# An eight-core decoder trunk: the first FFN on unnormalised input, ordered start DMAs, and the even mixer block by block

## The chip, the cores and the metric

The kernel runs on all 8 cores of one Trainium2 chip, in two dies of four cores. Each core computes one prompt of 2048 tokens and 16 sampled sequences of 8 tokens; the cores don't talk to one another. The metric is the device time of the slowest core in microseconds (us).

A program on all cores has a second, slower state: in some executions the cores of one die, or of both, get a lower TensorE clock (one run of start_only took 3130 us, with the cores of one die at 0.83). Only fast runs are compared here. Quoted ratios are the mean time of one kernel's fast runs over that of the other's of the same rounds, so they are not quite the ratio of the medians.

## The reference

Two layers, each with an FFN, a token mixer, a second FFN and a gated per-layer embedding. What matters here is the start and the mixer of layer 0:

```python
def rmsnorm(x, g):
    inv = lax.rsqrt(jnp.mean(x * x, axis=-1, keepdims=True) + NORM_EPS)
    return x * inv * g

def swiglu(h, w_gate_up, w_down):
    gu = h @ w_gate_up                      # width 2 * 2816
    gate, up = gu[..., :D_FF], gu[..., D_FF:]
    return (jax.nn.silu(gate) * up) @ w_down

x = x + 0.5 * swiglu(rmsnorm(x, norm_ffn[i, 0]), ...)
h = rmsnorm(x, norm_mix[i])
# even mixer
proj = h @ w_in                             # xa | va | ga, 512 channels each
pa = (causal multi-scale pooling of xa) @ pool_proj * pool_scale
u  = va * sigmoid(ga)
yb = silu(layernorm(causal_depthwise_conv31(u) + dw_bias))
x  = x + concat([pa, yb]) @ w_out
```

The first step of the change rests on an identity: `inv` is one number per token, so `rmsnorm(x, g) @ W` equals `inv * ((x * g) @ W)`. The matmul can start before `inv` is known, if its result is scaled afterwards.

## The kernel before

Channels lie on the 128 partitions, tokens along the free axis, in four blocks of 512 tokens (0 to 3) and one of 128 for the samples (`SB`). X is the residual in fp32, H the normalised input in bf16. Weights stream through a ring of 18 units, cast to bf16 by DMAs that the GpSimd queue issues. The program emits instructions in one order for all engines; `defer(delay, fn)` puts work off until the modelled PE time `pe_t` has moved on by `delay`, so that PE meets its operands ready. Every engine gets its own instructions in the order in which they were emitted; what this costs when one of them waits is seen below (DVE, 22.6 us). A "ones-matmul" multiplies by a constant matrix, so that PE forms a sum over the 128 partitions.

The start (cut):

```python
    for b in range(NB):
        for c in range(8):
            dma("sp" if b or c % 2 else "act", X[b][:, c, :], d_xT[...], f"x{b}_{c}")
    for i, b in ((0, 0), (4, 1), (5, 2), (6, 3), (7, 4)):      # weight i waits for all of x_b
        W.extra[i] = tuple((f"x{b}_{c}", 0, 16) for c in range(8))
    n0 = [Norm(b, "norm_ffn00") for b in range(NB)]            # squares, sum, ones-matmul, rsqrt,
    ...                                                        # eight normalising DVE instructions
```

The FFN takes four weight tiles through all five blocks first (the "lead"), then tile after tile. The even mixer (cut):

```python
        dma("pool", US[:, :, 0:30 * NS], d_stdw[:, :, :], "usem")      # conv state, cast to bf16
        dve_ts(US[:, :, 0:30 * NS], US[:, :, 0:30 * NS], 2.0, ALU.mult)
        def load_r(j, b):            # shifted copies of U for the convolution: 16 DMAs
            for s in range(4):
                for q in range(4):
                    ... ("sp", RALL[32*s:32*s+32, j, q, 0:L], U[32*q:32*q+32, j, BOFF[b]+s : ...])
        for (j, b) in lead_order(4, 3):            # value/gate projection, by tile
            ... u = (tanh(gate / 2) + 1) * value
            if b == 0: load_r(j, 0)
        for b in range(NB):
            xa(b)                                  # pooling projection
            if b == 0: conv(0)
        for b in range(NB):
            if b + 1 < NB: conv(b + 1)             # inside, per j: load_r(j, b + 2)
            pp(b)                                  # pool_proj, scaled copy by ACT
            ensure(("ln", b))
            out_proj(b, H, wo, gnext)
```

Of the kernel before, what the change touches and what calls it, by code (L numbers as in the profile page):

```python
# [215 lines left out]
class Sched:  # L216
# [14 lines left out]
    def regions(self, ap):  # L231
# [16 lines left out]
        return tuple(((arena, q), lo, hi) for q in range(p0 // 32, (p0 + pn - 1) // 32 + 1))  # L248
# [102 lines left out]
def build_program():  # L351
# [63 lines left out]
    PT = [alloc(f"pt{i}", [128, 2, 512], BF16) for i in range(2)]  # L415
# [140 lines left out]
    def mm(out, pairs, start=True, stop=True):  # L556
        n = len(pairs)
        mm_ops([(out, l, r, start and i == 0, stop and i == n - 1) for i, (l, r) in enumerate(pairs)])
        pe_t[0] += sum(max(width(r), 64) for _, r in pairs) / 2400.0
# [16 lines left out]
    class WStream:  # L576
        def __init__(self):
# [5 lines left out]
            self.extra = {}  # L583

# [20 lines left out]
        def pump(self):  # L605
            while self.pos < len(self.order):
# [23 lines left out]
    class Norm:  # L630
# [44 lines left out]
        def rsqrt(self):  # L675
# [4 lines left out]
            st = 1.0 if n == 512 else 0.3  # L680
# [11 lines left out]
            for c in range(8):  # L692
                defer(2.0 + st * c, mk(c), self.tag)

# [63 lines left out]
    def ffn(l, f, gnext, lead=3):  # L758
        for pi, part in enumerate(HPARTS):
# [4 lines left out]
            for oi, (j, b) in enumerate(order):  # L764
                n = BLK[b]
                ensure(("n", b))
# [6 lines left out]
                act(sg[:, 0:n], pg[:, 0:n], AF.Silu)  # L773
                bfree(pg)
                dve_tt(HID[b][:, j, :], pu[:, 0:n], sg[:, 0:n], ALU.mult)
                bfree(pu)
                sfree(sg)
# [47 lines left out]
    def even_mixer(gnext):  # L825
        dve_memset(U[:, :, 0:30], 0.0)
        dma("pool", US[:, :, 0:30 * NS], d_stdw[:, :, :], "usem")
        dve_ts(US[:, :, 0:30 * NS], US[:, :, 0:30 * NS], 2.0, ALU.mult)
        dve_memset(RALL[96:128, :, :, 536:RW], 0.0)
        dve_memset(PTAIL[:, :, :], 0.0)  # L830
        dma("sp", d_o_ps[:, :, 0:7 * NS], d_stp[:, :, 8 * NS:15 * NS], "osem")
        dma("sp", d_o_ds[:, :, 0:22 * NS], d_stdw[:, :, 8 * NS:30 * NS], "osem")

        def load_r(j, b):
            items = []
            for s in range(4):
                for q in range(4):
                    if b < SB:
                        L = 540 if s < 3 else 539
                        src = U[32 * q:32 * q + 32, j, BOFF[b] + s:BOFF[b] + s + L]  # L840
                    else:
                        L = RW if s < 3 else RW - NS
                        src = US[32 * q:32 * q + 32, j, s * NS:s * NS + L]
                    items.append(("sp", RALL[32 * s:32 * s + 32, j, q, 0:L], src))
            dma_group(items, f"rsem{j}")

        order, last = lead_order(4, 3)
        for oi, (j, b) in enumerate(order):
            n = BLK[b]
            ensure(("n", b))  # L850
            key = ("ine_vg", j)
            wt = kview(W.get(key), 8)
# [18 lines left out]
            if b == 0:  # L871
                load_r(j, 0)
            if last[j] == oi:
                W.done(key)
        dve_ts(O_DP[:, :, :], O_DP[:, :, :], 0.5, ALU.mult)
        dma("sp", d_o_dp[:, :, :], O_DP[:, :, :], "osem")

        
        def conv(b):
# [5 lines left out]
            p1, p2 = bank(), bank()  # L885
            tag = ("ln", b)

            def stats(j, vv):
                def f():
                    mm(p1[:, 0:n], [(ONESL[:, :], vv[:, 0, 0:n])], start=j == 0, stop=j == 3)  # L890
# [6 lines left out]
            def ln0():  # L897
                msq, rs = scr(), scr()
# [17 lines left out]
            for j in range(4):  # L916
# [7 lines left out]
                pe_t[0] += 8 * n / 2400.0  # L924
# [5 lines left out]
                defer(3.0, stats(j, vv), tag)  # L930
                if b + 1 < NB:
                    load_r(j, b + 1)

        def xa(b):
# [5 lines left out]
            pbs = []  # L940
            for c in range(4):
# [3 lines left out]
            for c in range(4):  # L945
                pb = pbs[c]
                w = 2 << c
                xe = scr()
                if is_s:
                    dma("sp", xe[:, 0:P], d_stp[:, c, :], f"stp{c}")  # L950
                else:
                    dve_copy(xe[:, 0:P], PTAIL[:, c, :])
# [28 lines left out]
                sfree(xe)  # L981
# [9 lines left out]
        wxa = [kview(W.get(("ine_xa", jj)), 8) for jj in range(2)]  # L991
        for b in range(NB):
            xa(b)
            if b == 0:
                conv(0)
        W.done(("ine_xa", 0))
# [213 lines left out]
```

## Time and profile before

| | |
|---|---|
| time | 2759.4 us median, 2756.4 to 2762.1 |
| TensorE (PE) busy | 94% of the span |
| PE's share of the chain of waits | 84% |
| lead of four FFN tiles ends | 127.4 us |
| even mixer | 554.5 to 852.9 us |

To see what is lost, I costed every matmul record at the spacing it has where PE is dense: 512 columns at 512 / 2.4 GHz + 2.5 ns = 215.8 ns, 128 columns at 55.8 ns. This is the rule in the Trainium skill, "TensorE: Matmul & The Clock Gate", Part 1; in this trace 218 matmuls fill the 40 us from 960 to 1000 us, which is what it gives for four blocks of 512 and one of 128. Four column-tiled convolution matmuls run side by side and count once. The sum is 2546.8 us of work. The span minus that sum is what I call *lost*: 212.4 us, of which 67.6 before the end of the lead, 110.0 in the even mixer, and 34.8 in all the rest (most of it at the end of the kernel, where nothing is left to overlap).

The page of before, its head and two of its strips; a digit is a fortieth of the span in tenths, and PEclk is the granted TensorE clock:

```profile
span 2759.2 us, 35204 instructions; the slowest of 8 cores (2746.5 to 2759.2 us)
PE 2592.8 (94%) x14347; PEld 1250.6 (45%) x14347; DVE 1151.8 (42%) x2089; ACT 701.3 (25%) x1248; POOL 87.4 (3%) x167
...
PE   4699999978759999999999999999999999999997
...
PEclk9899999998879999999999999999999999999999
```

The 9s are the dense stretches. The dips are the first two digits, digits 9 to 12 (the mixer) and the last one. 94% looks nearly full, yet the strip alone doesn't tell all: PE is also called busy when it runs at half clock. The by-window table of before, PE and granted clock (columns: stretch, length, busy us of PE, PEld, DVE, ACT, POOL, then PEclk, DMA share, GB/s), shows it:

```profile
60.00:80.00 20.00, 9.20 (x41) 3.79 (x39) 10.05 (x16) 8.85 (x15) 0.00 (x0) 0.77 0.32 54
80.00:100.00 20.00, 11.58 (x40) 4.55 (x41) 9.02 (x14) 3.07 (x4) 0.00 (x0) 0.64 0.00 0
```

From 80 to 100 us PE is busy for 11.58 us but does 40 matmuls, 8.6 us of work. The same skill page (section "What's actually happening") says that the clock falls to half after an idle window of about 3.4 us and comes back after as long a busy one. The trace agrees: from 575 to 580 us, in a gap of 14 us, the granted clock is 0.50; matmuls resume at 582.8 us, and the clock is 0.50 from 580 to 585 us, 0.90 from 585 to 590 and 1.00 after that. So a wait of several us is paid for twice.

Who made PE wait, before 140 us (us in total, times, longest). L538 is line 538 of the kernel; the names are its tiles: `ps` a PSUM bank, `h` the normalised input, `sq` squares, `scr` scratch, `rr` the shifted copies for the convolution, `u` and `us` their sources, `pt` the operands of the LayerNorm's sums:

```profile
PE ps L538 <- DVE sq_87 L507: 14.8, 1, 14.8
PE ps L538 <- DVE sq_88 L507: 11.0, 1, 11.0
PE ps L538 <- DVE h_49 L511: 9.1, 1, 9.1
PE ps L538 <- DVE h_48 L511: 8.0, 1, 8.0
```

and in the even mixer (520 to 900 us):

```profile
PE ps L538 <- DMA rr<-u: 20.8, 4, 7.5
PE ps L538 <- DMA rr<-us: 17.6, 2, 9.0
PE ps L538 <- DVE sq_86 L507: 14.1, 1, 14.1
PE ps L538 <- DVE pt_74 L525: 9.5, 2, 5.5
PE ps L538 <- ACT scr_91 L501: 6.4, 1, 6.4
```

All of the first list are products of the norm: sums of squares (`sq`) and normalised input (`h`). In the timeline of before, the first FFN matmul starts when the last of eight normalising instructions is done:

```profile
22.54 0.74 DVE L511 SCALAR_TENSOR_TENSOR h_48<-x_43,par,scr_92 128x512 bf16<-128x512 f32 x1
...
23.43 15.35 PE L538 MATMUL ps<-h_48,ring 128*128 128x512 bf16 x64 [8.01 <-DVE h_48 L511]
```

The wait for `sq_86` in the mixer is not DVE's slowness. DVE's own waits there (540 to 900 us) have one line that explains it: it stood for the convolution state, whose DMA was queued behind five weight tiles, with the norms' work queued behind it.

```profile
DVE us L516 <- DMA us<-st_dw: 22.6, 1, 22.6
```

And `rr<-u` are the shifted copies for the convolution. The issue of them by SP, from the timeline of SP (start, duration of the group, count), takes 0.66 us each and 42.6 us per block of 64:

```profile
638.47 42.58 SPq L562 DMA_DIRECT2D rr<-u  x64
...
692.60 85.14 SPq L562 DMA_DIRECT2D rr<-u  x128
```

### The profile page before, as it was taken

The numbers are of one execution on the slowest core, as the hardware profiler recorded it, in microseconds if no ns is written. First come the engines' busy times: TensorE is split into PE (matmuls) and PEld (weight loads), VectorE is DVE, ScalarE is ACT, GpSimd is POOL, SyncE is SP. The second block draws the span as 40 slices with busy tenths as digits, with TensorE's granted clock in tenths as the row PEclk, the third lists the DMA queues.
The fourth block names the chain that finished last, engine by engine and source line by source line (L and its number), as shares of the span: only waits on it lengthen the run. The fifth ranks groups of instructions, "written<-read, shape, count | busy, mean of one in ns | idle before, by whom it ended". The sixth has DMA issues, their size and how long they took to land.

```text
span 2759.2 us, 35204 instructions; the slowest of 8 cores (2746.5 to 2759.2 us)
## 1 busy us (share of the span) xinstructions
PE 2592.8 (94%) x14347; PEld 1250.6 (45%) x14347; DVE 1151.8 (42%) x2089; ACT 701.3 (25%) x1248; POOL 87.4 (3%) x167
## 2 busy tenths in 40 slices
PE   4699999978759999999999999999999999999997
PEld 1344544433224444444444445444444444444443
DVE  4422222736545222225872222227667612222587
ACT  3210011223443110112461101123333311011245
POOL 0000000000000000000000000000000000000000
PEclk9899999998879999999999999999999999999999
DMA  9121312043221220421312203121221221042113
GB/s 213 24 42 16 59 26 43 1 85 84 56 65 31 46 43 12 68 40 24 55 25 41 45 9 55 30 43 18 54 41 25 39 50 31 14 69 37 24 25 130
DMA packets 57203, 126.73 MB, mean 46 GB/s; under 512 B 13392, under 2 KB 28496, under 8 KB 56912
## 3 DMA queue, kind: packets, MB, share of 16 engines
q0 software_dynamic: 24112, 93.04, 20.2%
q1 hardware_dynamic: 32352, 30.39, 3.8%
q8 instruction: 113, 1.85, 0.3%
q10 hardware_dynamic: 576, 1.05, 0.1%
q14 instruction: 50, 0.41, 0.0%
HBM read 196.61 MB, written 10.62 MB: 75 GB/s over the span
## 4 chain that ended last, share of the span: by engine, by line
PE 84%; DVE 6%; SPq 4%; ACT 2%; issue 2%; DMA 1%; POOL 0%; DVEq 0%; ACTq 0%; POOLq 0%
PE ps L538 84%; SPq L562 4%; DMA us<-st_dw 1%; DVE h_50 L511 1%; ACT L499 1%; DVE h_49 L511 1%; DVE h_48 L511 1%; DVE scr_91 L507 0%; DVE h_51 L511 0%; DMA xscr_70<-st_sc 0%; DVE scr_93 L507 0%; DVE x_43 L511 0%; DVE scr_95 L507 0%; DVE x_46 L511 0%; DVE scr_92 L511 0%
## 5 line engine op out<-in xcount | busy, mean ns | idle before, releaser
L538 PE MATMUL ps<-h_49,ring 128*128 128x512 bf16 x1892 | 430.5, 381 | 11.6 <-DVE h_49 L511 9.1
L538 PE MATMUL ps<-h_48,ring 128*128 128x512 bf16 x1892 | 430.0, 381 | 10.5 <-DVE h_48 L511 8.0
L538 PE MATMUL ps<-h_50,ring 128*128 128x512 bf16 x1892 | 430.6, 382 | 8.5 <-DVE h_50 L511 6.1
L538 PE MATMUL ps<-h_51,ring 128*128 128x512 bf16 x1892 | 428.5, 381 | 1.6 <-ACT h_51 L501 1.6
L538 PEld LDWEIGHTS ps<-h_49,ring 128*128 128x128 bf16 x1892 | 185.8, 98 | 237.6 <-DVE h_49 L511 9.4
L538 PEld LDWEIGHTS ps<-h_50,ring 128*128 128x128 bf16 x1892 | 186.1, 98 | 236.1 <-DVE h_50 L511 6.6
L538 PEld LDWEIGHTS ps<-h_51,ring 128*128 128x128 bf16 x1892 | 185.5, 98 | 226.0 <-ACT h_51 L501 2.5
L538 PEld LDWEIGHTS ps<-h_48,ring 128*128 128x128 bf16 x1892 | 181.9, 98 | 215.5 <-issue 13.3
L501 ACT ACTIVATE scr_95<-ps 128x512 f32<-128x512 f32 (+1 forms) x130 | 74.2, 571 | 418.6 <-PE ps L538 395.2
L538 PE MATMUL ps<-hid_54,ring 128*128 128x512 bf16 x736 | 163.7, 379 | 0.0
L538 PE MATMUL ps<-hid_56,ring 128*128 128x512 bf16 x736 | 163.7, 379 | 0.0
L538 PE MATMUL ps<-hid_55,ring 128*128 128x512 bf16 x736 | 163.7, 379 | 0.0
L538 PE MATMUL ps<-hid_53,ring 128*128 128x512 bf16 x736 | 162.8, 379 | 0.0
L562 POOL DMA_DIRECT2D ring<-wts x152 | 80.9, 538 | 2423.9 <-PE ps L538 2327.9
L501 ACT ACTIVATE scr_92<-ps 128x512 f32<-128x512 f32 (+1 forms) x136 | 72.6, 534 | 326.7 <-PE ps L538 320.0
L501 ACT ACTIVATE scr_91<-ps 128x512 f32<-128x512 f32 (+1 forms) x133 | 74.7, 562 | 288.9 <-PE ps L538 282.3
L501 ACT ACTIVATE scr_94<-ps 128x512 f32<-128x512 f32 (+1 forms) x125 | 65.2, 521 | 311.5 <-PE ps L538 306.4
L538 PE MATMUL ps<-h_52,ring 128*128 128x128 bf16 x1892 | 128.3, 224 | 12.0 <-DVE scr_91 L511 4.0
L538 PEld LDWEIGHTS ps<-h_52,ring 128*128 128x128 bf16 x1892 | 118.1, 100 | 35.2 <-DVE scr_91 L511 4.3
L501 ACT ACTIVATE scr_93<-ps 128x512 f32<-128x512 f32 (+1 forms) x130 | 61.1, 470 | 217.7 <-PE ps L538 214.6
L507 DVE TENSOR_TENSOR hid_55<-ps,scr_91 128x512 bf16<-128x512 f32 x61 | 42.2, 692 | 167.9 <-PE ps L538 167.9
L538 PEld LDWEIGHTS ps<-hid_55,ring 128*128 128x128 bf16 x736 | 72.0, 98 | 86.6
(459 smaller groups left out, 2118.0 us busy)
## 6 DMA issues: line engine op xcount, KB each, us to landing
ring<-wts POOLq DMA_DIRECT2D x110, 512.0 KB, 8.8
ring<-wts POOLq DMA_DIRECT2D x40, 768.0 KB, 7.1
rr<-u SPq DMA_DIRECT2D x192, 33.8 KB, 1.9
rr<-u SPq DMA_DIRECT2D x64, 33.7 KB, 1.9
x_44<-xT SPq DMA_DIRECT2D x8, 256.0 KB, 10.4
x_45<-xT SPq DMA_DIRECT2D x8, 256.0 KB, 27.1
x_46<-xT SPq DMA_DIRECT2D x8, 256.0 KB, 16.6
yT<-x_43 SPq DMA_DIRECT2D x8, 256.0 KB, 2.1
```

What stands on the lines that cost most here:

```text
L499: e.preload_act_table_set(tset)
L501: return e.activation(out=out, in_=in_, func=func, **kw)
L507: S.op("dve", lambda e: e.tensor_tensor(out=out, in0=in0, in1=in1, op=op), reads=[in0, in1], writes=[out])
L511: S.op("dve", lambda e: e.scalar_tensor_tensor(out=out, in0=in0, scalar=scalar, in1=in1, op0=op0, op1=op1), reads=rd, writes=[out])
L538: ins = e.matmul(o_, l, r, start=st, stop=sp)
L562: S.op(eng, lambda e: e.dma_start(out=out, in_=in_), reads=[in_], writes=[out], dma_sem=sem, dma_total=total, extra_deps=extra)
```

## The change

Its intent: (1) let the first FFN of blocks 0 and 1 start from `X * gain`, and scale the gate before the SiLU and the product after it; (2) load in the order of need: four weights after x0, x1 after the third weight, further weights after all of X; (3) run the even mixer's projections by block rather than by tile, take the state load off DVE's way, and merge the convolution's loads from 320 DMAs to 80. With them go finer dependency tracking for the arena that holds U, two retuned constants of the deferral model, and, at the start, sums of squares of blocks 2 and 3 by eight ones-matmuls each on PE instead of adds on DVE.

```diff
-        pe_t[0] += sum(max(width(r), 64) for _, r in pairs) / 2400.0
+        pe_t[0] += sum(max(width(r), 64) + 6.5 for _, r in pairs) / 2400.0
...
-            st = 1.0 if n == 512 else 0.3
+            st = 0.7 if n == 512 else 0.3
...
+    class RawNorm:
+        def chunk(self, c, eng):
+            S.op(eng, lambda e: e.tensor_scalar(out=H[b][:, c, :], in0=X[b][:, c, :], scalar1=col, ...))
+            act(sq[:, 0:n], X[b][:, c, :], AF.Square)
+            ... eight ones-matmuls into one bank, then rsqrt into rs
...
+                if rw is not None:
+                    dve_tt(sg[:, 0:n], pg[:, 0:n], rw.rs[:, 0:n], ALU.mult)
+                    act(sg[:, 0:n], sg[:, 0:n], AF.Silu)
+                    def tail(...):                       # deferred by 1.5
+                        dve_tt(sg[:, 0:n], sg[:, 0:n], rs[:, 0:n], ALU.mult)
+                        dve_tt(HID[b][:, j, :], pu[:, 0:n], sg[:, 0:n], ALU.mult)
...
     def even_mixer(gnext):
-        dma("pool", US[:, :, 0:30 * NS], d_stdw[:, :, :], "usem")
-        dve_ts(US[:, :, 0:30 * NS], US[:, :, 0:30 * NS], 2.0, ALU.mult)
+        dma("sp", V[:, :, 0:30 * NS], d_stdw[:, :, :], "std")   # doubled into US later, deferred
...
-                        src = U[32 * q:32 * q + 32, j, BOFF[b] + s:BOFF[b] + s + L]
+                        src = U[32 * q:32 * q + 32, :, BOFF[b] + s:BOFF[b] + s + L]
-                    items.append(("sp", RALL[32 * s:32 * s + 32, j, q, 0:L], src))
+                    items.append(("act" if b > 1 and q % 2 else "sp", RALL[32 * s:32 * s + 32, :, q, 0:L], src))
...
-        order, last = lead_order(4, 3)
-        for oi, (j, b) in enumerate(order):
+        for b in (0, 1, 2, SB, 3):
+            for j in range(4):
+                vg(j, b)
+            xa(b)
+            if b == 0:
+                load_r(0)
+            if b == SB:
                 conv(0)
+                load_r(1)
...
             pp(b)
+            if b + 2 < NB:
+                load_r(b + 2)
             ensure(("ln", b))
             out_proj(b, H, wo, gnext)
...
-            dma("sp" if b or c % 2 else "act", X[b][:, c, :], d_xT[:, o_:o_ + n], f"x{b}_{c}")
+            dma("act" if b == 0 and c % 2 else "sp", X[b][:, c, :], d_xT[:, o_:o_ + n], f"x{b}_{c}",
+                extra=(("wsem4", 0, 16),) if b == 1 and c == 0 else ())     # x1 waits for the third weight
+    W.extra[0] = (("x0_2", 0, 16),)
+    W.extra[4] = tuple((f"x{SB}_{c}", 0, 16) for c in range(8))
...
+        raw[1].chunk(c, "pool")                  # block 1's multiplies on GpSimd, block 0's on DVE
...
+    n0 = [Norm(b, "norm_ffn00", "pe" if b < SB else "dve") for b in range(NB)]   # used for blocks 2, 3 and SB
```

More of the change, by code (lines that the diff above doesn't have):

```diff
@@ L247, in regions @@
         p0 = ap.offset // ps if ps > 0 else 0
-        return tuple(((arena, q), lo, hi) for q in range(p0 // 32, (p0 + pn - 1) // 32 + 1))
+        spans = [(lo, hi)]
+        if arena == "hid" and len(pat) == 3 and pat[1][1] > 1:
+            inner = ((pat[2][1] - 1) * pat[2][0] + 1) * es
+            if inner < pat[1][0] * es:
+                spans = [(lo + i * pat[1][0] * es, lo + i * pat[1][0] * es + inner) for i in range(pat[1][1])]
+        return tuple(((arena, q), a, b) for q in range(p0 // 32, (p0 + pn - 1) // 32 + 1) for a, b in spans)
     def _access(self, arena, lo, hi, ticket, is_write, deps):
@@ L414, in build_program @@
     RING = alloc("ring", [128, NRUNIT * RUNIT], BF16, "ring")
-    PT = [alloc(f"pt{i}", [128, 2, 512], BF16) for i in range(2)]
+    RSB = []
+    PT = []
+    for i in range(2):
+        RSB.append(at(f"rsb{i}", [128, 512], F32, "misc", cur[0]))
+        PT.append(alloc(f"pt{i}", [128, 2, 512], BF16))
     G = alloc("gram", [128, 2, 256], BF16)
@@ L583, in __init__ @@
             self.extra = {}
+            self.limit = 4
         def _place(self, k):
@@ L605, in pump @@
         def pump(self):
-            while self.pos < len(self.order):
+            while self.pos < self.limit:
                 k = self.order[self.pos]
@@ L693, in rsqrt, with __init__, add @@
                 defer(2.0 + st * c, mk(c), self.tag)
+    class RawNorm:
+        def __init__(self, b, gname):
+            self.b, self.gname, self.n = b, gname, BLK[b]
+            self.rs = RSB[b]
+            self.pb = None
+        def chunk(self, c, eng):
+            n, b = self.n, self.b
+            col = pcol(self.gname, c)
+            S.op(eng, lambda e: e.tensor_scalar(out=H[b][:, c, :], in0=X[b][:, c, :], scalar1=col, scalar2=None,
+                                                op0=ALU.mult), reads=[X[b][:, c, :], col], writes=[H[b][:, c, :]])
+            sq = SQ.get()
+            act(sq[:, 0:n], X[b][:, c, :], AF.Square)
+            def add():
+                if c == 0:
+                    self.pb = bank()
+                mm(self.pb[:, 0:n], [(ONES[:, :], sq[:, 0:n])], start=c == 0, stop=c == 7)
+                SQ.put(sq)
+                if c == 7:
+                    act(self.rs[:, 0:n], self.pb[:, 0:n], AF.Abs_reciprocal_sqrt, bias=NORM_EPS)
+                    bfree(self.pb)
+            defer(1.6, add, ("raw", b))
     def lead_order(nt, lead):
@@ L756, in emb_stats, with ffn @@
         defer(0.6, s0, tag)
-    def ffn(l, f, gnext, lead=3):
+    def ffn(l, f, gnext, lead=3, raw=()):
         for pi, part in enumerate(HPARTS):
@@ L765, in ffn @@
                 n = BLK[b]
-                ensure(("n", b))
+                rw = raw[b] if b < len(raw) else None
+                ensure(("n" if rw is None else "raw", b))
                 key = ("gu", l, f, part[j])
@@ L772, in ffn, with tail @@
                 sg = scr()
-                act(sg[:, 0:n], pg[:, 0:n], AF.Silu)
-                bfree(pg)
-                dve_tt(HID[b][:, j, :], pu[:, 0:n], sg[:, 0:n], ALU.mult)
-                bfree(pu)
-                sfree(sg)
+                if rw is not None:
+                    dve_tt(sg[:, 0:n], pg[:, 0:n], rw.rs[:, 0:n], ALU.mult)
+                    bfree(pg)
+                    act(sg[:, 0:n], sg[:, 0:n], AF.Silu)
+                    def tail(b=b, j=j, n=n, sg=sg, pu=pu, rs=rw.rs):
+                        dve_tt(sg[:, 0:n], sg[:, 0:n], rs[:, 0:n], ALU.mult)
+                        dve_tt(HID[b][:, j, :], pu[:, 0:n], sg[:, 0:n], ALU.mult)
+                        bfree(pu)
+                        sfree(sg)
+                    defer(1.5, tail)
+                else:
+                    act(sg[:, 0:n], pg[:, 0:n], AF.Silu)
+                    bfree(pg)
+                    dve_tt(HID[b][:, j, :], pu[:, 0:n], sg[:, 0:n], ALU.mult)
+                    bfree(pu)
+                    sfree(sg)
                 if last[j] == oi:
@@ L826, in even_mixer, with load_r @@
         dve_memset(U[:, :, 0:30], 0.0)
-        dma("pool", US[:, :, 0:30 * NS], d_stdw[:, :, :], "usem")
-        dve_ts(US[:, :, 0:30 * NS], US[:, :, 0:30 * NS], 2.0, ALU.mult)
-        dve_memset(RALL[96:128, :, :, 536:RW], 0.0)
         dve_memset(PTAIL[:, :, :], 0.0)
-        dma("sp", d_o_ps[:, :, 0:7 * NS], d_stp[:, :, 8 * NS:15 * NS], "osem")
-        dma("sp", d_o_ds[:, :, 0:22 * NS], d_stdw[:, :, 8 * NS:30 * NS], "osem")
-        def load_r(j, b):
+        def load_r(b):
             items = []
@@ L839, in load_r, with vg @@
                         L = 540 if s < 3 else 539
-                        src = U[32 * q:32 * q + 32, j, BOFF[b] + s:BOFF[b] + s + L]
+                        src = U[32 * q:32 * q + 32, :, BOFF[b] + s:BOFF[b] + s + L]
                     else:
                         L = RW if s < 3 else RW - NS
-                        src = US[32 * q:32 * q + 32, j, s * NS:s * NS + L]
-                    items.append(("sp", RALL[32 * s:32 * s + 32, j, q, 0:L], src))
-            dma_group(items, f"rsem{j}")
-        order, last = lead_order(4, 3)
-        for oi, (j, b) in enumerate(order):
+                        src = US[32 * q:32 * q + 32, :, s * NS:s * NS + L]
+                    items.append(("act" if b > 1 and q % 2 else "sp", RALL[32 * s:32 * s + 32, :, q, 0:L], src))
+            dma_group(items, "rsem")
+        def vg(j, b):
             n = BLK[b]
-            ensure(("n", b))
-            key = ("ine_vg", j)
-            wt = kview(W.get(key), 8)
+            wt = kview(W.get(("ine_vg", j)), 8)
             pv, pg = bank(), bank()
@@ L870, in even_mixer @@
             sfree(th)
-            if b == 0:
-                load_r(j, 0)
-            if last[j] == oi:
-                W.done(key)
-        dve_ts(O_DP[:, :, :], O_DP[:, :, :], 0.5, ALU.mult)
-        dma("sp", d_o_dp[:, :, :], O_DP[:, :, :], "osem")
         def conv(b):
@@ L884, in conv @@
             DG = W.get(("diag",)).rearrange("p (g m c) -> p g m c", g=16, m=8)
-            p1, p2 = bank(), bank()
+            pp_ = []
             tag = ("ln", b)
@@ L889, in f @@
                 def f():
+                    if j == 0:
+                        pp_[:] = [bank(), bank()]
+                    p1, p2 = pp_
                     mm(p1[:, 0:n], [(ONESL[:, :], vv[:, 0, 0:n])], start=j == 0, stop=j == 3)
@@ L897, in ln0 @@
             def ln0():
+                p1, p2 = pp_
                 msq, rs = scr(), scr()
@@ L923, in conv @@
                 mm_ops(ops)
-                pe_t[0] += 8 * n / 2400.0
+                pe_t[0] += 8 * (n + 512) / 2400.0
                 vv = LNP.get()
@@ L929, in conv @@
                 bfree(pb)
-                defer(3.0, stats(j, vv), tag)
-                if b + 1 < NB:
-                    load_r(j, b + 1)
+                defer(4.5, stats(j, vv), tag)
         def xa(b):
@@ L940, in xa @@
             pbs = []
+            wxa = [kview(W.get(("ine_xa", jj)), 8) for jj in range(2)]
             for c in range(4):
@@ L947, in xa @@
                 w = 2 << c
-                xe = scr()
-                if is_s:
-                    dma("sp", xe[:, 0:P], d_stp[:, c, :], f"stp{c}")
-                else:
+                xe = V[:, c, :] if is_s else scr()
+                if not is_s:
                     dve_copy(xe[:, 0:P], PTAIL[:, c, :])
@@ L980, in xa @@
                 sfree(src)
-                sfree(xe)
+                if not is_s:
+                    sfree(xe)
         def pp(b):
@@ L989, in pp, with state @@
                 bfree(pb)
-        wxa = [kview(W.get(("ine_xa", jj)), 8) for jj in range(2)]
-        for b in range(NB):
+        dma("sp", V[:, :, 0:30 * NS], d_stdw[:, :, :], "std")
+        def state(j):
+            dve_ts(US[:, j, 0:30 * NS], V[:, j, 0:30 * NS], 2.0, ALU.mult)
+            if j == 3:
+                dma("sp", V[:, :, 0:15 * NS], d_stp[:, :, :], "stp")
+        for b in (0, 1, 2, SB, 3):
+            ensure(("n", b))
+            if b == SB:
+                ensure(("us",))
+            for j in range(4):
+                vg(j, b)
             xa(b)
             if b == 0:
-                conv(0)
+                dve_memset(RALL[96:128, :, :, 536:RW], 0.0)
+                load_r(0)
+                for j in range(4):
+                    defer(3.0 * j, lambda j=j: state(j), ("us",))
+                dma("sp", d_o_ps[:, :, 0:7 * NS], d_stp[:, :, 8 * NS:15 * NS], "osem")
+                dma("sp", d_o_ds[:, :, 0:22 * NS], d_stdw[:, :, 8 * NS:30 * NS], "osem")
+            if b == SB:
+                conv(0)
+                load_r(1)
+        dve_ts(O_DP[:, :, :], O_DP[:, :, :], 0.5, ALU.mult)
+        dma("sp", d_o_dp[:, :, :], O_DP[:, :, :], "osem")
+        dma("sp", d_o_pp[:, :, :], PTAIL[:, :, 1:16], "osem")
+        for j in range(4):
+            W.done(("ine_vg", j))
         W.done(("ine_xa", 0))
         W.done(("ine_xa", 1))
-        dma("sp", d_o_pp[:, :, :], PTAIL[:, :, 1:16], "osem")
         wpp = kview(W.get(("pp",)), 4)
@@ L1090, in ple @@
             W.done(("pleg", l, ch))
+    dma("act", PAR[:, :], d_par[:, :], "psem")
     for b in range(NB):
@@ L1095, in build_program @@
             o_ = 8 * BOFF[b] + c * n
-            dma("sp" if b or c % 2 else "act", X[b][:, c, :], d_xT[:, o_:o_ + n], f"x{b}_{c}")
-        if b == 0:
-            dma("sp", PAR[:, :], d_par[:, :], "psem")
-    for i, b in ((0, 0), (4, 1), (5, 2), (6, 3), (7, 4)):
-        W.extra[i] = tuple((f"x{b}_{c}", 0, 16) for c in range(8))
+            dma("act" if b == 0 and c % 2 else "sp", X[b][:, c, :], d_xT[:, o_:o_ + n], f"x{b}_{c}",
+                extra=(("wsem4", 0, 16),) if b == 1 and c == 0 else ())
+    W.extra[0] = (("x0_2", 0, 16),)
+    W.extra[4] = tuple((f"x{SB}_{c}", 0, 16) for c in range(8))
     dve_memset(ONES[:, :], 1.0 / D)
-    n0 = [Norm(b, "norm_ffn00") for b in range(NB)]
-    for mo in range(8):
-        n0[0].chunk(mo)
+    raw = [RawNorm(b, "norm_ffn00") for b in range(2)]
+    for c in range(8):
+        raw[0].chunk(c, "dve")
         pe_t[0] += 0.8
         run_due()
+    pe_t[0] = 11.5
     dve_memset(ONESL[:, :], 1.0 / 512)
@@ L1111, in build_program, with chunk1 @@
         dve_memset(RC[:, t:t + 1], 1.0 / (t + 1))
-    for b in range(1, NB):
+    W.pump()
+    def chunk1(c):
+        raw[1].chunk(c, "pool")
+        if c == 7:
+            W.limit = len(wtiles)
+            W.pump()
+    for c in range(8):
+        defer(9.5 + 0.75 * c, lambda c=c: chunk1(c), ("raw", 1))
+    n0 = [Norm(b, "norm_ffn00", "pe" if b < SB else "dve") for b in range(NB)]
+    for b in range(2, NB):
         for mo in range(8):
-            defer(6.0 + 12.0 * (b - 1) + 0.9 * mo, lambda b=b, mo=mo: n0[b].chunk(mo), ("n", b))
+            defer((16.0, 24.0, 32.0)[b - 2] + (0.7, 0.9, 0.5)[b - 2] * mo, lambda b=b, mo=mo: n0[b].chunk(mo, 0.0), ("n", b))
     for l in range(2):
-        ffn(l, 0, f"norm_mix{l}", lead=4 if l == 0 else 3)
+        ffn(l, 0, f"norm_mix{l}", lead=4 if l == 0 else 3, raw=raw if l == 0 else ())
         if l == 0:
```

## The prediction

> **What bounds it.** PE is 94% busy and 84% of the chain of waits. I costed every matmul record at its dense spacing: in the by-window table, 960 to 1000 us, 218 matmuls fill 40 us, which fits 0.216 us for 512 columns and 0.056 for 128, the N / 2.4 GHz + 2.5 ns of the Trainium skill ("TensorE: Matmul & The Clock Gate", Part 1). That is 2546 us of work in 2759 (four column-tiled matmuls counted once), so 213 us are lost:
>
> - 0 to 140 us: 68 us. First FFN matmul at 23.4 us (timeline): it waits for x0, a squares/sum/rsqrt chain, eight normalising DVE instructions (last at 22.5) and the first weight (landed 22.3, behind x1). Later PE waits: h_49 9.1, sq_88 11.0 us. Idle gaps also cost clock (0.64 to 0.77 granted in three 20 us windows) (that section's gate).
> - Even mixer, 554 to 853 us: 110 us. One 14.1 us gap because DVE stood 22.6 us on the DMA us<-st_dw (DVE waits); 38.4 us on rr loads (PE waits); the rest is DVE/ACT latency in convolution and LayerNorm, at reduced clock. SP issues 320 rr DMAs at 0.63 us: 42.6 us per block where PE needs about 23.
> - Last 60 us: 21; everything else 15.
>
> **What changes.** Startup: blocks 0 and 1 need no rsqrt before the gate/up matmuls, and weights pass x1. x0 is in at about 12 us, the first weight at about 14, then one per 3.6 to 4.4 us. Block 0 runs 14 to 31 us at the pace of weights, block 1 from about 32 when x1 is in, blocks 2 and 3 follow with little gap. The four-tile lead should end near 84 us (before: 127). The price: two more DVE passes of 0.69 us per raw tile (2.1 us in a 3.45 us PE slot: hidden), GpSimd multiplies of about 0.8 us, about 6 us more ones-matmuls on PE. Startup loss 68 -> about 30.
>
> Mixer: the state DMA no longer stands in front of DVE. rr loads become 80, four times larger: 10 us of SP issue, or 5 on each of SP and ACT, hidden behind out_proj (13.8 us). vg plus xa of a block is 20.7 us of PE against about 12 of DVE. In the conv/out_proj loop I count per block 23.5 us PE, 24 DVE, 25 ACT with its DMA issues and table loads: balanced, so some loss stays. Mixer loss 110 -> about 30.
>
> Sum: 2546 + 6 + 30 + 30 + 35 (end and rest unchanged), or about 2642. All of it is on the critical path: PE is the chain in both stretches.
>
> **Predicted 2642 us, 8 in 10 between 2612 and 2685.** Chances: faster by over 2% 0.94, within 2% 0.05, slower 0.01.
>
> **What would show it.** First FFN matmul at 13 to 16 us; dense PE from about 82 us; no DVE wait on st_dw; PE waits on rr below 8 us; mixer (first vg matmul to the next FFN's first) 205 to 235 us instead of 298; conv/out_proj interval per block 24 to 30 us instead of 37 to 45; later FFNs unchanged to 5 us.
>
> **What would make it wrong.** Weight arrival: the mixer now needs four vg and two xa tiles within 21 us; they come one per 4 us once the down projection frees the ring. Out weights may come late. ACT stalled by its own DMA issues; DVE full in block 1 (8.3 us of raw tiles plus 5.5 of normalising in 13.8).

## The result, and the profile after

The changed kernel takes 2661.8 us (median of four runs: 2659.6, 2660.5, 2663.2 and 2685.0), 3.3% less; the ratio is 0.967, with a 95% interval of 0.961 to 0.972. In the run of 2685.0, cores 6 and 7 had a clock of 0.98 where the others had 0.99; without it the mean is 2661.1, 98.2 us below the 2759.3 of before. The 98 us is the number that I compare the experiments with.

```profile
span 2661.4 us, 34887 instructions; the slowest of 8 cores (2651.0 to 2661.4 us)
PE 2586.6 (97%) x14375; PEld 1249.3 (47%) x14375; DVE 1187.5 (45%) x2144; ACT 704.6 (26%) x1250; POOL 99.6 (4%) x174
...
PE   7999999999899999999999999999999999999997
...
PEclk9999999999899999999999999999999999999999
```

The two dips that the change aimed at are nearly gone from the strip; PE's busy time is 6 us less though it has 28 matmul records more, because fewer of them run at half clock. In the same accounting as before:

| us | before | after |
|---|---|---|
| work of all matmuls at dense spacing | 2546.8 | 2552.9 |
| first FFN matmul | 23.4 | 15.9 |
| end of the four-tile lead | 127.4 | 92.4 |
| lost up to there | 67.6 | 26.6 |
| even mixer | 298.4 | 228.6 |
| lost in it | 110.0 | 40.2 |
| lost in the rest | 34.8 | 41.7 |

The table is of the slowest core of each run. Over the six cores of each whose matmul records are complete, the mixer takes 288.1 to 298.4 us before and 222.0 to 228.6 after, and the rest loses 33.8 to 38.4 us before (median 34.4) and 38.6 to 41.7 after (median 38.8). A stage's figure of one core is good to some us only.

PE's waits over the whole of after, the longest five:

```profile
PE ps L547 <- ACT sq_88 L510: 6.6, 10, 1.5
PE ps L547 <- DVE pt_75 L534: 6.2, 3, 3.1
PE ps L547 <- DVE h_48 L714: 6.2, 1, 6.2
PE ps L547 <- DVE scr_95 L520: 5.5, 3, 3.4
PE ps L547 <- POOL h_49 L714: 4.2, 1, 4.2
```

No wait of PE for `rr` is left, and DVE doesn't wait for the state any more. The 6.2 us for `h_48` are the first idle stretch of the launch, while x0 and the parameters arrive (DVE's first multiply waited 4.3 us for the parameters' DMA); the first FFN matmul at 15.94 us then waited 2.17 us for its weights, not for a norm. `POOL h_49` is new; the timelines of PE and of GpSimd show it:

```profile
15.94 14.53 PE L547 MATMUL ps<-h_48,ring 128*128 128x512 bf16 x56 [2.17 <-DMA ring<-wts]
...
34.25 0.39 PE L547 MATMUL ps<-sq_88,ones 128*128 128x512 bf16 x1 [0.48 <-ACT sq_88 L510]
38.81 3.59 PE L547 MATMUL ps<-h_49,ring 128*128 128x512 bf16 x8 [4.18 <-POOL h_49 L714]
```

```profile
29.31 9.45 POOL L714 TENSOR_SCALAR h_49<-x_44,par 128x512 bf16<-128x512 f32 x6 [0.42 <-DMA x_44<-xT]
```

Six multiplies in a row took 9.45 us on GpSimd, 1.57 us each, and ended at 38.8 us; the last piece of x1 had landed at 33.4 us. After the gap of 4.2 us the next eight matmuls took 3.59 us instead of the 1.89 that eight take at 47.42 us, where PE is dense: half clock. The by-window table of after gives the granted clock (last but two columns) against the 0.64 to 0.77 of before:

```profile
40.00:60.00 20.00, 18.38 (x75) 7.74 (x73) 11.89 (x18) 12.40 (x20) 2.71 (x5) 0.89 0.84 181
60.00:80.00 20.00, 19.65 (x91) 8.78 (x92) 11.90 (x24) 10.84 (x20) 0.00 (x0) 1.00 0.37 59
```

In the mixer, SP issues a block's loads in 10.4 us where it took 42.6 (timeline of SP in after):

```profile
602.05 10.41 SPq L571 DMA_DIRECT2D rr<-u  x16
```

What is still lost lies in the convolution and output-projection loop, in small pieces of two kinds (timeline of PE in after): the sums for the LayerNorm wait for a cast, and the output projection waits for ACT's scaled copies of the pool branch.

```profile
632.52 1.04 PE L547 MATMUL ps<-pt_75,onesl 128*128 128x512 bf16 x2 [3.14 <-DVE pt_75 L534]
633.49 3.61 PE L547 MATMUL ps<-rr,ring 128*32 128x512 bf16 x32
...
641.22 3.63 PE L547 MATMUL ps<-h_48,ring 128*128 128x512 bf16 x16 [1.64 <-ACT h_48 L510]
```

The 32 convolution matmuls at 633.49 take 3.61 us at half clock; elsewhere 32 of them take 1.9.

### The profile page after: what moved, and what is told of

It reads as the page before. It is cut to its first block, busy times and chain, and to the rows that moved or that the text cites. A ratio compares the mean times of both kernels' runs of the same rounds, so it can differ in the third digit from the quotient of the medians.

```text
span 2661.4 us, 34887 instructions; the slowest of 8 cores (2651.0 to 2661.4 us)
## 1 busy us (share of the span) xinstructions
PE 2586.6 (97%) x14375; PEld 1249.3 (47%) x14375; DVE 1187.5 (45%) x2144; ACT 704.6 (26%) x1250; POOL 99.6 (4%) x174
## 4 chain that ended last, share of the span: by engine, by line
PE 85%; DVE 8%; ACT 3%; issue 1%; DMA 1%; ACTq 0%; POOL 0%; SPq 0%; DVEq 0%; POOLq 0%
PE ps L547 85%; DVE h_50 L520 1%; ACT L508 1%; DVE h_51 L520 1%; DMA ring<-wts 1%; DMA xscr_69<-st_sc 0%; DVE x_46 L520 0%; DVE h_49 L520 0%; DVE v L516 0%; DVE h_48 L520 0%; DVE x_45 L520 0%; DVE x_43 L520 0%; DVE scr_97 L516 0%; DVE scr_96 L516 0%; DVE scr_96 L520 0%
## 5 line engine op out<-in xcount | busy, mean ns | idle before, releaser
L547 PEld LDWEIGHTS ps<-h_49,ring 128*128 128x128 bf16 x1892 | 185.8, 98 | 231.9 <-issue 5.2
L547 PEld LDWEIGHTS ps<-h_50,ring 128*128 128x128 bf16 x1892 | 185.3, 98 | 230.6 <-ACT h_50 L510 2.6
L547 PEld LDWEIGHTS ps<-h_51,ring 128*128 128x128 bf16 x1892 | 185.6, 98 | 227.4 <-issue 3.5
L547 PEld LDWEIGHTS ps<-h_48,ring 128*128 128x128 bf16 x1892 | 182.2, 98 | 211.9 <-issue 8.1
L510 ACT ACTIVATE scr_97<-ps 128x512 f32<-128x512 f32 (+1 forms) x128 | 72.7, 568 | 265.4 <-PE ps L547 263.4
L510 ACT ACTIVATE scr_95<-ps 128x512 f32<-128x512 f32 (+1 forms) x116 | 59.8, 515 | 311.1 <-PE ps L547 307.2
L510 ACT ACTIVATE scr_93<-ps 128x512 f32<-128x512 f32 (+1 forms) x128 | 73.6, 575 | 250.7 <-PE ps L547 240.3
L547 PEld LDWEIGHTS ps<-h_52,ring 128*128 128x128 bf16 x1892 | 117.1, 100 | 32.5 <-DVE scr_95 L520 3.6
L510 ACT ACTIVATE scr_94<-ps 128x512 f32<-128x512 f32 (+1 forms) x108 | 54.3, 503 | 234.8 <-PE ps L547 229.7
L510 ACT ACTIVATE scr_96<-ps 128x512 f32<-128x512 f32 (+1 forms) x125 | 59.0, 472 | 207.6 <-PE ps L547 200.5
L547 PEld LDWEIGHTS ps<-hid_54,ring 128*128 128x128 bf16 x736 | 72.0, 98 | 86.9
L547 PEld LDWEIGHTS ps<-hid_56,ring 128*128 128x128 bf16 x736 | 72.1, 98 | 86.6
```

The lines of the kernel that those rows point to most:

```text
L510: return e.activation(out=out, in_=in_, func=func, **kw)
L547: ins = e.matmul(o_, l, r, start=st, stop=sp)
```

## The experiments

My theory was that the start and the mixer are two separate stretches in which PE waited, that each part of the change removes its own waits, and that the gains add. The rivals: the parts need one another; the retuned constants do much of it; or, within a part, one ingredient does all. All kernels below gave the right result. Times are means of fast runs, told as the difference to the mean of before's fast runs. The changed kernel stands at -98.2 us. But for the run of 2685.0, the fast runs of one kernel in one call lie within 4 us of each other (those of before within 6), so differences of 2 us between rows of different calls say nothing.

| kernel | fast runs | mean us | before | difference |
|---|---|---|---|---|
| start_only | 3 of 6 | 2726.5 | 2757.9 | -31.4 |
| mixer_only | 1 of 4 | 2698.6 | 2757.9 | -59.3 |
| model_only | 2 of 4 | 2763.4 | 2757.9 | +5.5 |
| dve_block1 | 4 of 5 | 2655.3 | 2757.9 | -102.6 |
| pp_first | 4 of 4 | 2666.0 | 2756.8 | -90.8 |
| raw_only | 4 of 4 | 2659.4 | 2756.8 | -97.4 |
| gate_only | 3 of 4 | 2699.0 | 2756.8 | -57.8 |
| state_front | 2 of 5 | 2672.8 | 2756.8 | -84.0 |
| load_split | 3 of 4 | 2713.1 | 2759.8 | -46.7 |
| all_sp | 2 of 4 | 2661.9 | 2759.8 | -97.9 |
| best_b | 4 of 5 | 2659.2 | 2759.8 | -100.6 |
| final | 4 of 6 | 2648.2 | 2758.1 | -109.9 |

### start_only: the changed start with the mixer of before

```diff
 (after, with the whole function even_mixer of before put back)
```

> The changed kernel with the even mixer of before. Theory (the two parts are separate, each a stretch in which PE waits): about 2725 us (2718 to 2732), the mixer again about 298 us from its first vg matmul, and this plus mixer_only gives the whole gain of 98 us within 8 us. Rival (the parts need one another, or the retuned delays of deferred work give much of it): the two gains miss the sum by over 15 us.

-31.4 us. The trace has the lead's end at 93.0 us (after: 92.4) and a mixer of 294.3 us.

### mixer_only: the changed mixer with the start of before

```diff
 (after, with the start section of before put back)
-        ffn(l, 0, f"norm_mix{l}", lead=4 if l == 0 else 3, raw=raw if l == 0 else ())
+        ffn(l, 0, f"norm_mix{l}", lead=4 if l == 0 else 3, raw=())
```

> The changed kernel with the start of before (normalised blocks 0 and 1, ungated DMAs). Theory: about 2692 us (2685 to 2700), the mixer 225 to 235 us, the start as before (dense PE from about 127 us). Rival as for start_only.

-59.3 us from a single fast run, so the size is good to a few us only. The trace of that run agrees with it: the mixer takes 226.9 us, the lead ends at 129.1 us. The two gains sum to 90.7 us of the 98.2.

### model_only: the two retuned constants alone

```diff
 (before)
+        pe_t[0] += sum(max(width(r), 64) + 6.5 for _, r in pairs) / 2400.0
+            st = 0.7 if n == 512 else 0.3
```

> The kernel before with only the two retuned constants of the deferral model (6.5 cycles more per matmul, 0.7 instead of 1.0 between normalising instructions). Theory: nothing, 2753 to 2763 us. Rival (the retuning is a part of the gain): 2745 us or less.

+5.5 us (two fast runs): not a part of the gain but a small loss, just over the 2763 that I gave as the upper end for "nothing". Start_only and mixer_only both carry it. Taken out of each, the start gives 36.9 and the mixer 64.8 us; sum 101.7, less 5.5 once, 96.2 against 98.2. So the parts add. (The finer tracking of U's arena rides in start_only and in mixer_only too and was not run alone.) The trace says where the 5.5 us arise: outside the start and the mixer 40.6 us are lost instead of 34.8 (medians over the complete cores: 40.1 and 34.4), in a dozen short waits for ACT's squares in the later norms (after 860 us):

```profile
PE ps L538 <- ACT sq L501: 11.4, 12, 2.0
```

In before, the waits of that kind sum to 6.1 us (2.8, 1.2, 1.1 and 1.0).

### raw_only and gate_only: which half of the start?

```diff
 (raw_only: after, with the DMA order of before)
+            dma("sp" if b or c % 2 else "act", X[b][:, c, :], d_xT[:, o_:o_ + n], f"x{b}_{c}")
+    for i, b in ((0, 0), (4, 1), (5, 2), (6, 3), (7, 4)):
+        W.extra[i] = tuple((f"x{b}_{c}", 0, 16) for c in range(8))
 (gate_only: after, with the norms of before for all blocks, raw=())
```

> The changed kernel with the DMA order of before at the start (raw blocks 0 and 1 kept). Theory: weight 0 lands at about 22 us behind x1, so the first FFN matmul is at about 22 us and not 16; x1 is early, so block 1 follows block 0 without a gap; 2 to 12 us slower than the changed kernel. Rival (the order of DMAs is what made the start fast): 20 us or more slower.

> The changed kernel with the norms of before at the start, DMAs gated. Theory: both blocks need the chain of squares, sum, rsqrt and eight normalising instructions again, and x1 now comes late (33 us): first FFN matmul at 20 to 23 us, 25 to 40 us slower than the changed kernel, so no gain from the gating alone. Rival: the gating gives most of the start's gain, under 15 us slower.

Without the ordered DMAs the kernel is as fast as with them: -97.4 against -98.2 us. Both of my theories for raw_only missed; I had expected 2 to 12 us more. With the ordered DMAs but without the new norms, 40 us of the gain are gone, which is the whole of the start's 37 (my theory, at its upper edge). With mixer_only (old norms, old order, -59.3) the four runs are a two-by-two table: the norms give 38 to 40 us under either order of the DMAs; the order changes 0.8 us with the new norms and -1.5 with the old ones, which is noise (mixer_only is one run). But "the norms" are two things: gate_only also puts the sums of blocks 2 and 3 back from PE to DVE. Of its 62.4 us of waits, 40.1 stand before blocks 0 and 1 and 22.3 before the later blocks; in after, all waits before blocks 2 and 3 make 2 us. How much of this the raw norms of blocks 0 and 1 give alone was not run. The lead ends at 132.1 us, later than the 127.4 of before, because x1 comes later and its norm chain with it. The first FFN matmul comes at 29.3 us, not at the 20 to 23 that I expected: DVE stood 6.9 us (from 20.9 to 27.8 us) on an add for block 1, whose x1 was late, with the last normalising instruction of block 0 behind it. PE's waits in gate_only up to 132 us are two lines:

```profile
PE ps L547 <- DVE h L520: 41.8, 5, 13.8
PE ps L547 <- DVE sq L516: 20.6, 3, 14.9
```

Why raw_only loses nothing: the first weight lands at 22.4 us behind x1, and PE waits for it.

```profile
PE ps L547 <- DMA ring<-wts: 9.0, 1, 9.0
```

But then x1 is in at 22.5 us, so block 1 follows block 0 without a gap, and PE runs dense from 22.5 us but for one wait of 1.7 us and some half clock at its start. With the ordered DMAs PE starts at 15.9, and loses the 6.6 us again at block 1: 4.2 us of waiting, half a us just before it, and 13 matmuls at a spacing of 0.427 us instead of 0.216 after it (2.8 us). Weights are no part of this: from 20.6 to 33.4 us PE runs without a gap. The lead ends at 91.2 us in one and 92.4 in the other. The order moved the wait; it did not shorten the sum. Both runs have block 1's multiplies on GpSimd. In raw_only that is hidden, as x1 is early; with them on DVE the ordered start is the faster one (dve_block1: 87.8, final: 85.5). Raw_only with DVE was not run.

### dve_block1: block 1's multiplies on DVE

```diff
-        raw[1].chunk(c, "pool")
+        raw[1].chunk(c, "dve")
```

> The changed kernel with the eight multiplies of block 1 on the vector engine instead of GpSimd. Theory: they took 1.57 us each on GpSimd, and the last ended at 38.8 us while x1 was in at 33.4; on the vector engine (0.44 us each) block 1 starts at about 34.5 us, the 4.2 us wait and the half clock after it go, 4 to 8 us faster than the changed kernel (2654 to 2658). Rival (x1 and the weights set the pace, or the vector engine then delays the tails of block 0): within 2 us of it.

-102.6 us, 4.4 us better than the changed kernel, and the lead ends at 87.8 us instead of 92.4. A multiply takes 0.48 us on DVE. GpSimd was the wrong engine for this.

### state_front: the state load back at the head of the mixer

```diff
+        dma("pool", US[:, :, 0:30 * NS], d_stdw[:, :, :], "usem")
+        dve_ts(US[:, :, 0:30 * NS], US[:, :, 0:30 * NS], 2.0, ALU.mult)
-        dma("sp", V[:, :, 0:30 * NS], d_stdw[:, :, :], "std")
-            dve_ts(US[:, j, 0:30 * NS], V[:, j, 0:30 * NS], 2.0, ALU.mult)
```

> The changed kernel with the state load of before at the head of the mixer (cast by the GpSimd queue behind five weights, doubled at once by the vector engine). Theory: the vector engine stands about 20 us there again, all PSUM banks and scratch tiles fill, PE stops for 12 to 18 us: 12 to 20 us slower. Rival (the new order has enough slack): under 5 us slower.

-84.0 us, so the load at the head costs 14 us (two fast runs). The profiled run had die 0 slow; its core 5, on the undisturbed die, has a mixer of 234.4 us, against 222.0 on core 5 of the changed kernel (the four cores of that die: 10 to 12 us longer). DVE's waits and PE's timeline on core 5:

```profile
DVE us L525 <- DMA us<-st_dw: 20.4, 1, 20.4
```

```profile
543.76 0.29 PE L547 MATMUL ps<-sq,ones 128*128 128x128 bf16 x1 [10.89 <-DVE sq L516]
```

### load_split: 320 loads again, in the new order

```diff
-            items = []                       # one DMA for four channel groups, SP and ACT
-                        src = U[32 * q:32 * q + 32, :, ...]
+            for j in range(4):               # one DMA per channel group, all from SP
+                        src = U[32 * q:32 * q + 32, j, ...]
```

> The changed kernel with each merged convolution load split into four per-channel-group loads again (320 DMAs of 34 KB instead of 80 of 135 KB, all from SP; the new order is kept). Theory: the issue time of the DMAs was a large part of the old mixer loss: 42 us of SP issue per block do not fit behind the 28 us of a block, PE waits on rr loads 8 to 15 us per block for blocks 2, 3 and the sample block, 25 to 45 us slower than the changed kernel. Rival (the new order alone hides the loads): under 8 us slower.

-46.7 us: the split costs 51 us, more than I had expected, and 51 of the mixer's 65 us of gain are gone. It moves the same bytes from the same places at the same points of the program. SP is busy issuing without a break from 600 to 771 us, and PE waits for it in the mixer:

```profile
PE ps L547 <- DMA rr<-u: 37.1, 6, 10.2
PE ps L547 <- DMA rr<-us: 17.4, 2, 8.8
```

```profile
643.79 85.73 SPq L571 DMA_DIRECT2D rr<-u  x128
```

A DMA takes SP 0.67 us to issue whether it carries 34 KB here or 135 KB in after (10.41 us for 16); the medians are 0.59 and 0.61 us, though some of the larger ones took up to 1.4.

Load_split also says something of the block order, which no run tests alone. It has the new order and the state load moved, with 320 loads, and gains 46.7 us; start_only, with the whole old mixer, gains 31.4. The difference of 15 us is hardly more than the 14 that state_front gives to the state load. If these gains add, which is not shown, the order by itself is worth about 1 us; that is an estimate from these three times.

### all_sp: no loads from ACT

```diff
-                    items.append(("act" if b > 1 and q % 2 else "sp", RALL[...], src))
+                    items.append(("sp", RALL[...], src))
```

> The changed kernel with all convolution loads issued by SP, none by ACT (still 80 merged DMAs). Theory: ACT no longer stands 6.3 us per block in DMA issue just when it owes the squares of the residual, but PE's waits in the loop are for the pool copies, which come earlier in ACT's queue, so the time falls by 0 to 4 us only. Rival 1 (ACT's issue time is on the critical path): 6 us or more faster. Rival 2 (one queue is too slow for sixteen loads, 10 us of issue): PE waits on rr appear and it is slower.

-97.9 us (two fast runs): no difference. Once merged, sixteen loads fit on one queue, and ACT's issuing (7.4 to 7.8 us per block in the trace of after, not the 6.3 of the expectation) was not on the path. Together with load_split this says that from SP alone 320 DMAs cost 51 us against 80. Whether 320 over two queues would have been hidden was not run: all_sp shows no effect of the queue for the 80 merged loads only.

### pp_first: the pool projection ahead of the convolution

```diff
         for b in range(NB):
+            pp(b)
             if b + 1 < NB:
                 conv(b + 1)
-            pp(b)
```

> The changed kernel with the pool projection of a block issued before the convolution of the next block instead of after it. Theory: PE then no longer waits for the scaled pool copies (1.6, 2.0, 2.1, 1.9 and 3.2 us in the wait list) nor runs the first eight output projection matmuls at half clock: 10 to 16 us faster than the changed kernel (2646 to 2652). Rival (the loop is bound by the vector or scalar engine, and the wait moves elsewhere): within 3 us of it.

-90.8 us: 7 us *slower* than the changed kernel, outside both theories, though the rival (the wait moves elsewhere) had the mechanism. The waits for `h_48` to `h_51` went, as meant, and a larger one came. PE's waits from 620 to 760 us:

```profile
PE ps L547 <- DVE sq L516: 17.9, 3, 6.5
```

That is the ones-matmul of the norm of the block just projected: it now sat between the second and third group of the convolution, before DVE had its sum ready.

### best_b: both waits attacked

```diff
 (pp_first, dve_block1 and all_sp together, and:)
-        nm = Norm(b, gnext)                                  # in out_proj
+        nm = Norm(b, gnext, "dve", 8.0 if src is H else 2.5) # its ones-matmul deferred by 8 instead of 2.5
```

> Block 1's multiplies on the vector engine, the pool projection before the next convolution, all loads from SP, and the ones matmul of each block's norm after the out projection deferred further (8 us of modelled PE time instead of 2.5), as pp_first stood 6 us per block waiting for that sum. Theory: both waits of the loop go; 10 to 18 us faster than the changed kernel (2643 to 2651). Rival (the vector engine is full in the loop: 22 of 28 us busy, with chains): no faster than dve_block1 alone (2655 or more).

-100.6 us, no faster than dve_block1 alone (-102.6): the rival's time was right. The `sq` wait is gone, and others took its place (PE's waits, 510 to 760 us):

```profile
PE ps L547 <- DVE pt L534: 6.8, 2, 4.3
PE ps L547 <- ACT pt L510: 6.2, 2, 3.8
PE ps L547 <- ACT h L510: 5.6, 1, 5.6
```

The period of the loop, from one block's convolution to the next, stayed at 27.7 to 29.8 us (changed kernel: 28.2 to 31.6) where PE has about 23.5 us of work (205 matmuls from 655.5 to 683.8 us in after, at dense spacing). Three orders of the same work gave three different waits and nearly one period. I take this for a chain through the three engines (convolution, cast, sums, LayerNorm, convolution, with one V buffer and two buffers for the sums), but I only argue it; a kernel with more buffers, which would show it, doesn't fit: 32 bytes of SBUF per partition are free.

### final: three edits that the runs pointed to

```diff
-                extra=(("wsem4", 0, 16),) if b == 1 and c == 0 else ())
+                extra=(("wsem2", 0, 16),) if b == 1 and c == 0 else ())   # x1 after the second weight
-        raw[1].chunk(c, "pool")
+        raw[1].chunk(c, "dve")
+            tune[:] = [0.0, 1.0]            # after even_mixer: the old deferral constants again
```

> Three edits on the changed kernel: block 1's multiplies on the vector engine (as dve_block1), x1 released by the second weight instead of the third, and the old constants of the deferral model after the even mixer, as model_only lost more outside the mixer than the kernel before (40.6 against 34.8 us of PE time) by waits on ACT's squares. Theory: lead of four tiles ends 1 to 4 us before dve_block1's 87.8 us; loss outside start and mixer falls from 41.6 to 35 to 38 us; 5 to 9 us faster than dve_block1's 2655 us (2646 to 2650). Rival (x1's gate and the deferral constants are noise): within 2 us of dve_block1.

2648.2 us, -109.9: the best of all, 11.7 us better than the changed kernel and 7.3 better than dve_block1, as expected. The lead ends at 85.5 us, and 34.6 us are lost outside the start and the mixer, the figure of before (dve_block1: 87.8 and 41.6). So the trace shows a gain in each of the two places that the further edits touch, but the edits were not run apart. The ratio to before is 0.960 (0.958 to 0.961).

## Why the prediction was right

The time was inside the range (2612 to 2685) and the direction and its size were right, 20 us above the point. Point by point:

- **The shape of the loss was right.** All of the gain lies in the two stretches named, and nothing else got faster. The gains of the two parts add up (96 of 98 us). The terms explain the 19 us between the point and the profiled run: 5.0 by the slip below, 10.2 in the mixer, 6.7 in the rest, 0.9 of work, and 3.4 less in the start.
- **The point had a slip of addition.** 2546 + 6 + 30 + 30 + 35 is 2647, not 2642. Of the 19 us between 2642 and the profiled 2661, that is 5.
- **The mixer's loss: 30 predicted, 40 measured** (34 to 40 over the six cores with complete records). "Balanced, so some loss stays" was the right warning; its size was short by up to 10 us. The length, 228.6 us, was in the range given (205 to 235). What the prediction named as its parts was shown: state_front gives 14 us to the state load, load_split 51 us to the number of loads. The block order, which the title names, has no run of its own (see load_split). The interval per block was 26.3 to 31.6 us, where I had said 24 to 30.
- **The start's loss: 30 predicted, 26.6 measured, but by another path.** "And weights pass x1" was given as half of the reason. raw_only and gate_only show that in this kernel it is worth nothing with the new norms or without them: the new norms do it all (with the sums of blocks 2 and 3 on PE, which the prediction names only by their cost). It seems to pay once block 1 is off GpSimd (dve_block1, final). A GpSimd multiply was put at half of what it takes, 1.57 us. Block 0 "at the pace of weights" was wrong too: it waited for the first weight and for none after it. For the multiplies, with the half clock after the gap, and DVE's `h_50` 1.8 us late (the "DVE full in block 1" of the list of doubts), the lead ended at 92.4 us and not at 84. These two figures of the prediction also contradict each other: the lead has 65.8 us of work (92.4 - 26.6), so a lead that ends at 84 loses 18 us, and a loss of 30 ends it at 96. What was measured lies between. That the loss came so near to 30 is in part luck. The first matmul at 15.9 us was inside 13 to 16.
- **"Later FFNs unchanged to 5 us" held only just, if at all:** 41.7 us lost in the rest instead of 34.8 on the slowest cores, 38.8 instead of 34.4 in the median of the complete ones. The prediction took the two retuned constants for nothing. model_only shows that they cost about 5 us, and final gets them back.
- **Of the doubts,** late weights in the mixer did not come true (no wait of PE for the ring is among its longer ones), and ACT's own DMA issue did not matter (all_sp).

## What to carry to other kernels

Cost the matmuls at their dense spacing and subtract: that names the few stretches in which PE loses time, and there a change can be worth something. In such a stretch count DMAs and not only bytes: here the issuing queue took about the same time for a small one as for one four times larger (0.59 and 0.61 us in the median, and 51 us of the kernel's time), and ask of every in-order engine what stands behind an instruction that waits for a DMA. Reordering the loop moved the wait in both tries here instead of removing it (pp_first, best_b), and so did reordering the loads of the start as long as block 1 then waited for a slow engine (raw_only); taking a dependency out of the chain, as the new norms do, is what shortened it.

## What the Trainium skill lacked or had wrong

- "GPSIMD Engine Reference", section 4.1: one-input elementwise work is called roughly line-rate there. Here a one-input multiply of 128x512, fp32 to bf16 with a per-partition scalar, took 1.57 us on GpSimd (six in a row in after) and 0.48 us on DVE (all sixteen of dve_block1), about three times as long.
- "DMA: Bandwidth & Descriptors", section "Issuing engines are not separate DMA queues": it calls the sequencer's time to start a DMA usually small relative to the DMA itself. For SBUF-to-SBUF copies of 34 KB it was the limit: 0.66 us to issue each on SP, 51 us of the kernel's time in load_split. For the 80 merged loads a second issuing engine brought nothing (all_sp: 0.3 us of difference); for the 320 small ones that was not tried.
- "ScalarE: Activation LUTs", section "What ACT_TABLE_LOAD costs": 1.28 us of load agrees with the trace, but it adds a drain of 1.38 us to each switch. Here the next activation starts right after the load (an activation ends at 612.43 us, load at 612.44 for 1.28, next activation at 613.74; 43 of the 61 loads of after stand so between two activations), so a switch costs about 1.3 us.
- "TensorE: Matmul & The Clock Gate", Part 1: it advises to budget 1.95 GHz for dense matmuls on all cores. The fast runs of all kernels here held a mean granted clock of 0.97 to 1.00 on all eight cores; one die or both at a lower clock, down to 0.81, appeared in 27 of the 88 executions of the experiments (model_only: 3222 us with one die at 0.81 to 0.82), and the page doesn't say that the state differs from run to run of one program.
- No page tells what a delay model for issuing dependent work should be tuned to; a change of 6.5 cycles per matmul and of 0.3 us per instruction cost 5.5 us (model_only).
